# Issuing each group's value product one step later than its last transposes, in a mixed attention and retention layer

## The chip, the cores and the metric

The kernel runs on one core of a Trainium2 chip. The metric is the device time of one execution in microseconds, as the median of several runs. The engines are named as in the profile: PE is the matrix engine (PEld its weight loads), DVE the vector engine, ACT the scalar engine, POOL the general engine, and SP the engine that issues most of the DMAs.

## The reference, cut to what matters

One layer over 1024 rows of width 1024, batch 1. One input projection feeds three kinds of heads and a gate; their outputs are gated, projected back and added to the input, and a norm ends it.

```
u = rms_norm(x); proj = u @ w_in          # split into q, k, v of the groups, index keys, gate
o_a: 6 heads, causal; a = softmax(q1 k1) - lam * softmax(q2 k2); o = a @ v; norm per head
o_b: 6 heads; an index score picks 256 keys for each query (top-k); softmax over these; o = p @ v
o_c: 4 heads of retention over chunks of 128
y = silu(gate) * concat(o_a, o_b, o_c);  out = rms_norm(x + y @ w_out)
```

The change touches o_a and o_b. Both make, for each block of 128 queries, a row-wise softmax over the keys so far, transpose it (the value product wants the keys on the partitions) and multiply it with the values.

## The kernel before, in words

`diff(pair)` computes two heads of o_a, `dsa(pair, half)` two heads of o_b for one half of the queries. Both drive one generator, `attend`, with four stages of their own: `head` loads a head's queries and keys from DRAM into tiles `st`, `scores` multiplies them into a PSUM tile `pS` (L718, L787, L788), `soft` takes the row maximum on DVE out of `pS` (L729, L795) and the exponential on ACT (L731, L796), and `comb` normalises (in `diff` on POOL, L744, and DVE, L747).

`attend` walks over steps. A step is one block i of 128 queries of one head; two blocks (i = 2g and 2g+1) make a group g. Its pipeline is written out by hand. At time t it issues the scores of step t, then the transposes of step t-2 (L678, 128x128 each, up to four into one PSUM tile `pB`, L676) and the copy of each such tile into the group's SBUF tile `pt` (L679, helper lines L113 and L115, nearly always on ACT), then `comb` of step t-1 and `soft` of step t. If step t-2 was the second of its group, it then issues the group's value product (L693), which reads `pt` and the values `v`, and writes another `pB` tile. A value product has 2i+1 instructions: 15, 11, 7 or 3 for i = 7, 5, 3, 1. Groups run from the last to the first in `diff` (3, 2, 1, 0), and (1, 0) or (3, 2) in `dsa`.

All `pB` tiles share two PSUM buffers, all `pS` tiles two others, and `pt` has two. A tile of a buffer can be written only when the readers of the tile that had it before are done: for transposes that is the copy into `pt`, for a value product the copy `yo` (L519, L115) in `diff` or the multiplication by the gate `gt` (L825) in `dsa`.

What is written here is the order of issue. A scheduler that knows the dependencies, the buffers and an estimate of durations then sets the order on each engine; every engine works through its own queue in that order. Other generators are mixed with `attend` by weights: the matrix products of the input projection (`gemm`, L130 to L132, and L347 to L349), the top-k search (`topk`, on DVE and ACT, L443 to L464), the tie rule (`ties`), retention, and the output projection (`project`, L1003 to L1005). The weights apply to the costs that the generators yield, so that a generator with another number of yields is also mixed differently.

The lines that matter most are the buffers:

```
def pS(self): ... tag="S", bufs=2
def pB(self, shape=(128, 512)): ... tag="B", bufs=2
pts[g, a] = self.sb.tile([128, NB, W], F, name=self.name("pt"), tag="pt", bufs=2)
```

Of the kernel before, what the change touches and what calls it, by code (L numbers as in the profile page):

```python
# [68 lines left out]
class Trunk:  # L69
# [582 lines left out]
    def attend(self, pair, stages, GB=2, groups=(3, 2, 1, 0)):  # L652
        nc = self.nc
        steps = [(a, g, i) for a in range(2) for g in groups
                 for i in range(g * GB, g * GB + GB)]
        head, scores, soft, comb = stages
        pts, val = {}, {}
        W = GB * 128
        N = len(steps)
        hd = {}  # L660
        for t in range(N + 2):
            if t < N:
                a, g, i = steps[t]
                if a not in hd:
                    hd[a] = head(a)
                val[t] = scores(hd[a], i)
            if t >= 2:
                a, g, i = steps[t - 2]
                pr = val.pop(t - 2)
                if (g, a) not in pts:  # L670
                    pts[g, a] = self.sb.tile([128, NB, W], F, name=self.name("pt"), tag="pt", bufs=2)
                pt = pts[g, a]
                qo = (i - g * GB) * 128
                for k0 in range(0, i + 1, 4):
                    nk = min(4, i + 1 - k0)
                    p = self.pB((128, 4, 128))  # L676
                    for k in range(nk):
                        nc.tensor.transpose(p[:, k], pr[:, (k0 + k) * 128:(k0 + k + 1) * 128], self.ident)  # L678
                    self.cp(self.evac_eng[k0 // 4], pt[:, k0:k0 + nk, qo:qo + 128], p[:, :nk])  # L679
            if 0 <= t - 1 < N:  # L680
                val[t - 1] = comb(val[t - 1])
            if t < N:
                val[t] = soft(steps[t][2], val[t])
            if t >= 2 and steps[t - 2][2] % GB == GB - 1:
                a, g, i = steps[t - 2]
                o = self.pB((128, 128))
                h = 2 * pair + a
                vals = [self.v[:, k, h * 64:(h + 1) * 64] for k in range(i + 1)]
                with self.tc.manual_schedule(engines={mybir.EngineType.PE}):
                    for k in (i, *range(i)):  # L690
                        for u in (1, 0):
                            if k < i or u:
                                self.last = nc.tensor.matmul(  # L693
                                    o[u * 64:(u + 1) * 64], vals[k], pts[g, a][:, k, u * 128:(u + 1) * 128],
                                    start=k == (i if u else 0), stop=k == i - 1, skip_group_check=True)
                yield 0.5, (a, g, o)
            yield (steps[min(t, N - 1)][2] + 1) / 4.5, None
# [354 lines left out]
```

## Time and profile before

| what | value |
|---|---|
| median of 3 runs | 768.53 us (767.16 to 770.72) |
| the profiled execution, its own time | 772.95 us |
| its span, first to last instruction | 771.2 us |
| PE busy | 718.2 us, 93% |
| DVE busy | 559.9 us, 73% |
| ACT busy | 458.6 us, 59% |
| mean granted clock of PE | 0.973 |

PE is the engine with the most busy time. Its records overlap, since matrix products are pipelined: products of 128x512 show 0.39 us each and start 0.23 us apart. A product with a 32-bit operand that takes two passes has two records, so a value product of 15 instructions is shown as x30. The execution that was profiled took 4.42 us more than the median of the runs.

### The profile page before, as it was taken

Reading aid. Unit: us, or ns where it says so; the run is one execution under the profiler, and the core shown is the slowest. Engines: PE = TensorE matmul, PEld = TensorE weight load, DVE = VectorE, ACT = ScalarE, POOL = GpSimd, SP = SyncE. Lnnn points to the kernel's source line nnn. Section 1 sums busy time; section 2 is a strip of 40 time slices with the busy share of each in tenths; the row PEclk is TensorE's granted clock in tenths of the full one; section 3 lists DMA queues with packets and bytes.
Section 4 is the critical chain, followed back from the end, with each engine's and each line's share of the span. In section 5 each row is a group of like instructions: output and inputs, shape, how many; then the busy total and the mean of one; then the engine's idle time right before and its main releaser. Section 6 shows DMA issues by size and latency. Waiting matters only on the chain.

```text
span 771.2 us, 12824 instructions
## 1 busy us (share of the span) xinstructions
PE 718.2 (93%) x4266; PEld 591.1 (77%) x4266; DVE 559.9 (73%) x1315; ACT 458.6 (59%) x1002; POOL 310.4 (40%) x343
## 2 busy tenths in 40 slices
PE   6999999999989999978889889999978999999996
PEld 5986788887878988756767668989756887777884
DVE  3684577989999989999889986426657775654443
ACT  4762555489687877786845655533355665653332
POOL 6422122434424539447347787337633332120000
PEclk9999999999999999999899989999979999999998
DMA  9716455472484344451383685565579964413441
GB/s 337 255 28 178 137 159 142 111 191 79 118 202 109 99 132 113 114 144 31 91 239 108 172 229 167 145 203 165 177 212 272 251 203 113 132 34 106 137 166 55
DMA packets 93618, 116.73 MB, mean 151 GB/s; under 512 B 11120, under 2 KB 62704, under 8 KB 93424
## 3 DMA queue, kind: packets, MB, share of 16 engines
q1 hardware_dynamic: 91152, 111.94, 50.8%
q10 hardware_dynamic: 2400, 3.97, 1.4%
q8 instruction: 34, 0.56, 0.3%
q14 instruction: 32, 0.26, 0.1%
HBM read 79.17 MB, written 36.18 MB: 150 GB/s over the span
## 4 chain that ended last, share of the span: by engine, by line
PE 62%; DVE 13%; DMA 8%; issue 7%; ACT 4%; POOL 4%; SPq 2%; ACTq 0%; DVEq 0%; POOLq 0%
PE pG L130 6%; PE pG L131 6%; PE pG L132 6%; PE pB L693 5%; PE pB L678 4%; PE pG L1003 4%; PE pG L1004 4%; PE pG L1005 4%; PE pS L272 3%; PE pG L347 2%; DVE jv L443 2%; PE pG L349 2%; PE pG L348 2%; PE pS L409 2%; PE pS L408 2%
## 5 line engine op out<-in xcount | busy, mean ns | idle before, releaser
L130 PE MATMUL pG<-uh,wh 128*128 128x512 f32 x352 | 142.5, 405 | 4.5 <-DVE gt L894 2.1
L132 PE MATMUL pG<-uh,wl 128*128 128x512 f32 x352 | 141.2, 401 | 1.7 <-POOL wl L123 1.7
L131 PE MATMUL pG<-ul,wh 128*128 128x512 f32 x352 | 140.4, 399 | 1.3 <-DVE ul L255 1.3
L123 POOL TENSOR_TENSOR wl<-wr,wh 128x512 fp32r<-128x512 f32 x56 | 79.9, 1443 | 84.4 <-PE pG L131 73.8
L457 ACT ACTIVATE ja<-sc,tk_c 128x896 int8<-128x896 f32 (+2 forms) x93 | 83.3, 896 | 22.3 <-DVE tk_c L464 16.5
L113 ACT ACTIVATE pt<-pB 128x512 f32<-128x512 f32 (+2 forms) x120 | 58.9, 496 | 41.9 <-PE pB L678 41.7
L130 PEld LDWEIGHTS pG<-uh,wh 128*128 128x128 f32 x352 | 67.5, 192 | 19.3 <-DVE gt L894 2.4
L132 PEld LDWEIGHTS pG<-uh,wl 128*128 128x128 f32 x352 | 67.4, 192 | 16.7 <-POOL wl L123 2.5
L131 PEld LDWEIGHTS pG<-ul,wh 128*128 128x128 f32 x352 | 67.4, 191 | 15.5 <-DVE ul L255 3.3
L678 PE MATMUL pB<-ident,pp 128*128 128x128 f32 x432 | 73.4, 288 | 4.6 <-DVE gt L825 1.9
L693 PE MATMUL pB<-pt,v 128*64 128x128 f32 x864 | 68.0, 294 | 7.4 <-ACT pt L113 6.8
L693 PEld LDWEIGHTS pB<-pt,v 128*64 128x64 f32 x864 | 55.3, 143 | 18.9 <-ACT pt L113 9.5
L443 DVE TENSOR_SCALAR_CACHE_REDUCE jv<-sc,tk_c 128x640 bf16<-128x640 f32 (+4 forms) x81 | 69.1, 853 | 0.9
L119 POOL TENSOR_SCALAR wh<-wr 128x512 fp32r<-128x512 f32 x56 | 40.3, 723 | 69.9 <-DMA wr<-in_w_in_dram 50.8
L678 PEld LDWEIGHTS pB<-ident,pp 128*128 128x128 f32 x432 | 51.7, 145 | 20.4 <-issue 8.5
L744 POOL TENSOR_SCALAR pq<-pq,mx 128x896 f32<-128x896 f32 (+7 forms) x48 | 39.2, 816 | 58.5 <-DVE mx L743 46.1
L347 PE MATMUL pG<-wh,uh 128*128 128x256 f32 x192 | 55.4, 290 | 0.7 <-POOL wh L119 0.7
L411 ACT ACTIVATE pp<-pS 128x1024 f32<-128x1024 f32 (+5 forms) x48 | 36.5, 760 | 31.5 <-PE pS L409 31.5
L348 PE MATMUL pG<-wl,uh 128*128 128x256 f32 x192 | 55.0, 287 | 0.0
L349 PE MATMUL pG<-wh,ul 128*128 128x256 f32 x192 | 54.4, 284 | 0.0
L747 DVE SCALAR_TENSOR_TENSOR pp<-pp,mx,pq 128x896 f32<-128x896 f32 (+7 forms) x48 | 51.1, 1065 | 4.4 <-POOL pq L744 3.6
L416 DVE SCALAR_TENSOR_TENSOR sc<-pp,iw,sc 128x1024 f32<-128x1024 f32 (+5 forms) x42 | 43.5, 1048 | 14.6 <-ACT pp L411 14.2
(234 smaller groups left out, 1731.4 us busy)
## 6 DMA issues: line engine op xcount, KB each, us to landing
wr<-in_w_in_dram SPq DMA_DIRECT2D x56, 256.0 KB, 3.1
st<-qdq SPq DMA_DIRECT2D x24, 256.0 KB, 4.2
st<-qkk SPq DMA_DIRECT2D x18, 256.0 KB, 6.1
qiq<-hl SPq DMA_DIRECT2D x16, 256.0 KB, 3.5
st<-qiq SPq DMA_DIRECT2D x8, 512.0 KB, 3.4
wr<-in_w_out_dram SPq DMA_DIRECT2D x16, 256.0 KB, 3.3
xr<-in_x_dram SPq DMA_DIRECT2D x8, 512.0 KB, 3.6
yr<-yd SPq DMA_DIRECT2D x7, 512.0 KB, 4.1
```

Source lines behind the costliest of these rows:

```text
L113: self.nc.scalar.activation(out, in_, AF.Copy)
L123: (self.nc.vector if e2 == "v" else self.nc.gpsimd).tensor_tensor(lo, src, hi.bitcast(F), OP.subtract)
L130: mm(ps, wh, xh, start=start, stop=False)
L131: mm(ps, wh, xl, start=False, stop=False)
L132: mm(ps, wl, xh, start=False, stop=stop)
L347: mm(ps, uh, hs[k], start=k == 0, stop=False)
L348: mm(ps, uh, ls[k], start=False, stop=False)
L349: mm(ps, ul, hs[k], start=False, stop=k == KC - 1)
L443: nc.vector.tensor_scalar(jv[:, :nv[b]], hb if b == 7 and bit >= 16 else sc[b], t, 0.0, op0=op, op1=OP.add, accum_out=cnt[:, j:j + 1])
L457: nc.scalar.activation(ja[:, :nv[b]], sc[b], AF.Sign, bias=cut(b), scale=-1.0, accum_out=cnt[:, cols[b]:cols[b] + 1])
L678: nc.tensor.transpose(p[:, k], pr[:, (k0 + k) * 128:(k0 + k + 1) * 128], self.ident)
L693: self.last = nc.tensor.matmul(o[u * 64:(u + 1) * 64], vals[k], pts[g, a][:, k, u * 128:(u + 1) * 128], start=k == (i if u else 0), stop=k ...
```

## The change

The loop of `attend` runs one step longer. Where the value product of a group was issued in the same step as the group's last transposes, the group is now only noted (`done`), and its product is issued at the same place of the next step (`ready`), that is behind the scores, the transposes, `comb` and `soft` of that next step. `L` names the distance of two steps between scores and transposes, which stays. Each `attend` yields once more.

```diff
-        for t in range(N + 2):
+        L = 2
+        done = None
+        for t in range(N + L + 1):
             if t < N:
                 a, g, i = steps[t]
                 if a not in hd:
                     hd[a] = head(a)
                 val[t] = scores(hd[a], i)
-            if t >= 2:
-                a, g, i = steps[t - 2]
-                pr = val.pop(t - 2)
+            ready, done = done, None
+            if L <= t < N + L:
+                a, g, i = steps[t - L]
+                pr = val.pop(t - L)
                 if (g, a) not in pts:
                     pts[g, a] = self.sb.tile([128, NB, W], F, name=self.name("pt"), tag="pt", bufs=2)
                 pt = pts[g, a]
...
                     self.cp(self.evac_eng[k0 // 4], pt[:, k0:k0 + nk, qo:qo + 128], p[:, :nk])
+                if i % GB == GB - 1:
+                    done = (a, g, i)
             if 0 <= t - 1 < N:
                 val[t - 1] = comb(val[t - 1])
             if t < N:
                 val[t] = soft(steps[t][2], val[t])
-            if t >= 2 and steps[t - 2][2] % GB == GB - 1:
-                a, g, i = steps[t - 2]
+            if ready:
+                a, g, i = ready
                 o = self.pB((128, 128))
```

Both programs hold the same instructions; what differs is their order on every engine. Three places are shown. In the change's rows the lines behind L661 have moved by a few: L681 is the transposes (L678 before), L698 the value product (L693), L723 the scores (L718).

**Place 1** is PE at the first value product (15 instructions) of the second head of `diff(1)`. The names `pG` are products of other generators. Before:

```order
L678 MATMUL pB_3346<-ident,pp_3215 128x128 x4
L678 MATMUL pB_3352<-ident,pp_3215 128x128 x4
L718 MATMUL pS_3463<-st_3128,st_3125 128x384
L132 MATMUL pG_3573<-uh,wl_3488 128x512
L130 MATMUL pG_3573<-uh,wh_3487 128x512
L131 MATMUL pG_3573<-ul,wh_3487 128x512
L132 MATMUL pG_3573<-uh,wl_3488 128x512
L718 MATMUL pS_3510<-st_3121,st_3118 128x512
L693 MATMUL pB_3370<-pt_3298,v_158 64x128 x15
L678 MATMUL pB_3466<-ident,pp_3319 128x128 x4
```

And in the change:

```order
L681 MATMUL pB_3377<-ident,pp_3230 128x128 x4
L681 MATMUL pB_3383<-ident,pp_3230 128x128 x4
L723 MATMUL pS_3438<-st_3106,st_3103 128x384
L506 MATMUL pG_3425<-hl_3422,ct 128x512
L723 MATMUL pS_3440<-st_3113,st_3110 128x384
L681 MATMUL pB_3443<-ident,pp_3308 128x128 x4
L681 MATMUL pB_3449<-ident,pp_3308 128x128
L723 MATMUL pS_3516<-st_3106,st_3103 128x512
L698 MATMUL pB_3464<-pt_3287,v_158 64x128 x15
L723 MATMUL pS_3518<-st_3113,st_3110 128x512
```

The five transposes of the next step now stand ahead of the product, and the four products of the input projection that stood between have gone elsewhere. The product takes the PSUM buffer of the four transposes `pB_3443` before it.

**Place 2** is PE at the second value product (11 instructions) of the first head of `diff(1)`. Before, ten products of the input projection stand between its last two transposes and the score product shown first here:

```order
L131 MATMUL pG_3288<-ul,wh_3278 128x512
L132 MATMUL pG_3288<-uh,wl_3279 128x512
L718 MATMUL pS_3071<-st_2484,st_2481 128x256
L693 MATMUL pB_2977<-pt_2882,v_158 64x128 x11
L678 MATMUL pB_3039<-ident,pp_2901 128x128 x3
L678 MATMUL pB_3073<-ident,pp_2974 128x128 x4
```

In the change twenty-one products of the input projection and a score product stand between those two transposes and the three of the next step, shown in the third row:

```order
L130 MATMUL pG_3233<-uh,wh_3170 128x512
L681 MATMUL pB_3020<-ident,pp_2878 128x128 x3
L698 MATMUL pB_3037<-pt_2859,v_158 64x128 x11
L723 MATMUL pS_3117<-st_3106,st_3103 128x512
L723 MATMUL pS_3117<-st_3106,st_3103 128x384
```

The product moved behind the next step's transposes and further away from its own.

**Place 3** is the queue of SP around the loads of the second head of `diff(1)` (`st`, L383). The stores `qsq` (L370) write a projection that `dsa` needs later, out of tiles `hl` that POOL fills. Before:

```order
L522 DMA yo_64<-yo_2790 64x128 x2
L370 DMA qsq_3169<-hl_3238 64x2x512 x2
L383 DMA st_3118<-qdq_1854 64x1024 x2
L370 DMA qsq_3169<-hl_3272 64x2x512 x2
L383 DMA st_3121<-qdk_1647 64x1024
L383 DMA st_3121<-qdk_1647 32x1024 x2
L530 DMA f_2906<-gd_1398 128x512
L383 DMA st_3125<-qdq_1854 64x1024 x2
```

And in the change:

```order
L522 DMA yo_64<-yo_2900 64x128 x2
L383 DMA st_3103<-qdq_1890 64x1024 x2
L900 DMA gr<-gt_3163 128x512
L383 DMA st_3106<-qdk_1673 64x1024
L383 DMA st_3106<-qdk_1673 32x1024 x2
L383 DMA st_3110<-qdq_1890 64x1024 x2
L383 DMA st_3113<-qdk_1673 64x1024
L530 DMA f_2921<-gd_1398 128x512
```

The loads no longer stand behind the two stores.

## Rows read from the trace of the kernel before

**Rows 1.** The page's busy times and its slices (PEclk is the granted clock).

```profile
PE 718.2 (93%) x4266; PEld 591.1 (77%) x4266; DVE 559.9 (73%) x1315; ACT 458.6 (59%) x1002; POOL 310.4 (40%) x343
...
PEclk9999999999999999999899989999979999999998
```

**Rows 2.** Busy us of each engine by stretch, with clock and DMA share.

```profile
core 0: us, PE busy (x) PEld busy (x) DVE busy (x) ACT busy (x) POOL busy (x), PEclk, DMA share, GB/s
...
300.00:350.00 50.00, 42.61 (x244) 32.56 (x242) 47.95 (x118) 41.74 (x99) 28.99 (x32) 1.00 0.47 128
350.00:400.00 50.00, 43.25 (x244) 35.09 (x242) 43.93 (x119) 33.12 (x78) 24.58 (x27) 0.93 0.43 111
```

**Rows 3.** What PE waited for: us in total, times, longest.

```profile
PE pB L693 <- ACT pt L113: 6.8, 3, 3.5
...
PE pS L718 <- DVE mx L729: 4.6, 8, 0.9
```

**Rows 4.** PE in order of time around place 1: start, us, work, idle before.

```profile
362.36 1.03 PE L678 MATMUL pB<-ident,pp 128*128 128x128 f32 x8
...
364.12 0.40 PE L132 MATMUL pG<-uh,wl 128*128 128x512 f32 x1
364.35 0.39 PE L130 MATMUL pG<-uh,wh 128*128 128x512 f32 x1
...
365.04 0.46 PE L718 MATMUL pS<-st,st 128*128 128x512 f32 x1
369.01 3.67 PE L693 MATMUL pB<-pt,v 128*64 128x128 f32 x30 [3.51 <-ACT pt L113]
372.61 1.12 PE L678 MATMUL pB<-ident,pp 128*128 128x128 f32 x4
```

**Rows 5.** ACT in the same stretch.

```profile
363.82 0.94 ACT L731 ACTIVATE pp<-pp,mx 128x768 f32<-128x768 f32 x1 [3.53 <-DVE mx L729]
...
366.35 1.03 ACT L457 ACTIVATE ja<-sc,tk_c 128x896 int8<-128x896 f32 x1
...
367.90 1.06 ACT L113 ACTIVATE pt<-pB 128x512 f32<-128x512 f32 x2
```

**Rows 6.** DVE behind it.

```profile
374.16 0.29 DVE L729 CUSTOM_DVE_ANT_0 pq<-pS,cb 128x128 f32<-128x128 f32 x1 [1.74 <-PE pS L718]
...
379.91 0.69 DVE L729 CUSTOM_DVE_ANT_0 pp<-pS,cb 128x512 f32<-128x512 f32 x1 [0.93 <-PE pB L678]
```

**Rows 7.** PE clock in two stretches, columns as in the second group.

```profile
366.95:373.80 6.85, 4.79 (x35) 4.46 (x36) 5.43 (x14) 6.63 (x18) 2.71 (x4) 0.50 0.38 107
...
561.50:571.80 10.30, 9.25 (x40) 6.55 (x41) 6.28 (x25) 6.33 (x20) 4.29 (x4) 0.50 0.59 180
```

**Rows 8.** PE around place 2.

```profile
309.83 1.96 PE L693 MATMUL pB<-pt,v 128*64 128x128 f32 x30
...
325.30 0.38 PE L678 MATMUL pB<-ident,pp 128*128 128x128 f32 x2
...
327.85 0.28 PE L718 MATMUL pS<-st,st 128*128 128x256 f32 x1
330.90 1.52 PE L693 MATMUL pB<-pt,v 128*64 128x128 f32 x22 [2.78 <-ACT pt L113]
...
335.22 0.65 PE L718 MATMUL pS<-st,st 128*128 128x512 f32 x2 [1.02 <-DMA st<-qdk]
```

**Rows 9.** SP's issues in the same stretch (place 3).

```profile
327.76 1.28 SPq L370 DMA_DIRECT2D qsq<-hl  x2
329.09 2.15 SPq L383 DMA_DIRECT2D st<-qdk  x3
```

**Rows 10.** PE at a value product of the first half of `dsa`.

```profile
550.58 0.65 PE L693 MATMUL pB<-pt,v 128*64 128x128 f32 x6 [0.47 <-ACT pt L113]
```

**Rows 11.** PE at the last value product.

```profile
708.39 1.06 PE L678 MATMUL pB<-ident,pp 128*128 128x128 f32 x7
710.07 1.50 PE L693 MATMUL pB<-pt,v 128*64 128x128 f32 x22 [0.61 <-DVE pt L115]
```

**Rows 12.** ACT in the same stretch.

```profile
709.14 0.60 ACT L113 ACTIVATE pt<-pB 128x512 f32<-128x512 f32 x1 [0.17 <-PE pB L678]
```

## The prediction, made before the changed kernel ran

> **What bounds the kernel now.** I read the page first: PE is busy for 93% of the span and DVE for 73% [rows 1]. The reader should not stop at the average. The table by stretch shows that between 300 and 400 us DVE is the fuller engine at first: 47.95 of 50 us, with PE at 42.61 [rows 2]. There the softmaxes of `diff` share DVE with the top-k search, and PE idles because its scores and copies come late. Later it is PE that is full.
>
> Then I asked what PE waits for. The wait that the change is about, the value product waiting for the copy of its transposes, heads the list with 6.8 us, but that is three waits [rows 3]: 2.78 us at 330.90 [rows 8], 3.51 us at 369.01 [rows 4], and 0.47 us at 550.58 [rows 10]. A fourth, for a copy that DVE made, is 0.61 us at 710.07 [rows 11]. Together 2.78 + 3.51 + 0.47 + 0.61 = 7.37 us, or 1.0% of the time. There are 60 value products; the other 56 found their copy made, since the order had already put other work between.
>
> Why was the copy late at 369 us? The eight transposes ended at 362.36 + 1.03 = 363.39; the copies ran from 367.90 to 368.96 [rows 4, 5]. That is 5.57 us, of which the copies are 1.06. ACT was not short of time: it had stood 3.53 us for an exponential whose row maximum DVE had not made, and only then went through its queue, in which the copies come behind that exponential and the top-k's `ja` [rows 5]. The cause is DVE, and a product issued later doesn't change it. With no such queue the copy ends soon: at the last group it ran from 709.14 to 709.74, right behind transposes that ended by 709.45 [rows 11, 12].
>
> After the wait the PE clock is at its lower level, 1.2 GHz: 0.50 granted from 366.95 to 373.80, with 4.79 us of work in it [rows 7]. The same kind of product took 3.67 us there [rows 4] and 1.96 us at the full clock [rows 8]. Half of 4.79, 2.4 us, is the price.
>
> **The change part by part.** *Work.* No instruction is added or removed but for the engine of a few `pt` copies, each about 0.6 us [rows 12]: zero. What moves is order, on every engine.
>
> *Place 1, the 3.51 us wait.* In the change the product is behind the next step's five transposes. It writes the PSUM buffer that four of these have just filled, so it must wait until they are copied away. Only one transpose and one score product are between, about 0.1 + 0.23 = 0.34 us by the spacing of products (364.12 to 364.35 [rows 4]; a transpose of 128 columns is taken as less than half of that). Before, four products of the projection and two score products stood between. So the product still waits for a copy on ACT, of later transposes, behind other exponentials. The wait lies between 0.6 - 0.34 = 0.3 us (the quick copy) and 5.57 - 0.34 = 5.2 us (the slow one). The row at this very place is the nearest, so I keep 3.5 us: term 0, between -3.2 and +1.7. What of it reaches the end is what it takes from DVE, which stood 1.74 and 0.93 us after it [rows 6]: a gain of at most 2.7 us, not the 3.51.
>
> *Place 2, the 2.78 us wait.* Here the order does help. The copy was done at 330.90, which is 330.90 - 325.68 = 5.2 us after the transposes. In the change twenty-one projection products, a score product and three transposes stand between, (21 + 1) x 0.23 + 0.3 = 5.4 us, and the buffer it needs is an older one. I expect the wait gone. But DVE was busy for 47.95 of 50 us around it [rows 2], so the idle time of PE was not what set the end there: I take 0, between -2.8 and 0.
>
> *Place 3.* The loads of the next head stood behind `qsq` stores that left at 327.76 [rows 9], and PE waited 1.02 us for them [rows 8]. Now they go first. Under the same DVE cover: 0, between -1.0 and 0.
>
> *The two small waits.* At 710 us PE is the full engine, and in the change twenty-five products of the output projection precede the last value product; 0.61 is saved on the path. The one at 550.58 us is taken as saved too: together -1.1 us, at the worst 0.
>
> *Waits added.* Counted over the whole order, two of the six 15-instruction products of `diff` now have less than 0.8 us of work between the transposes whose buffer they take and themselves: place 1 and its like in the first head of `diff(2)` (three projection products, about 0.7 us). The second can cost up to 5.57 - 0.7 = 4.9 us, and at place 1 the five transposes follow the eight of the step before with only three small products between, so that they wait too. Under DVE's cover I take 0 for both; 4.9 is the upper end. Queued behind a waiting product are the scores of later steps, for which DVE waits; that is how it would reach the end.
>
> In the first half of `dsa`, where steps are short, the distance from the transposes whose copy or buffer gates a product to that product is about 0.2 to 1.3 us in most cases before and 0.3 to 1.2 after: the change moves nothing there. The step that each `attend` runs more only emits the product that was held back.
>
> *The sum.* 0 + 0 + 0 - 1.1 + 0 = -1.1 us on the profiled execution's 772.95, so 771.9. That execution was 4.42 us above the median of 768.53; on the median it is **767.4 us**.
>
> **The rivals.** *Faster, the waits really go.* For it: place 2 loses its wait outright, and the stretch at half clock begins in the wait at place 1. Against it: DVE is full at both, and place 1 keeps its gate. All gains together: 7.4 for the waits, 2.4 for the clock, 1.0 for the loads, 10.8 us, 757.7; what is more likely of it is DVE's 2.7 on top of the 1.1, plus one or two, so 762 to 764.
>
> *Slower, the product waits for the buffer it takes.* With two `pB` buffers a product issued behind the next step's transposes takes the buffer these have just filled. At place 1 and at its like PE would stand 1.7 us more and 4.9 us, and one more stretch at half clock costs 2.4: 9 us, 777.5. It decides as soon as DVE runs dry behind these products, as it did at 374.16 [rows 6]; while DVE has other work queued it costs nothing. For it: the order at place 1, with 0.34 us between. Against it: only two of 24 products in `diff` stand so.
>
> The Trainium skill, TensorE: Matmul & The Clock Gate, section "A second HAM failure mode: psum-queue depth-cycling", says that a matrix engine that cycles through PSUM buffers and idles a little between groups loses more than the idle time, since its clock falls and rises again. The half clock behind the wait at place 1 agrees [rows 7]; by that rule each wait for a buffer is dearer than its length, and this rival would be the likelier.
>
> *The change doesn't do what it says.* The scheduler reorders anyway, so a product issued later may stand no further from its copy, as in the first half of `dsa`. Then the time is 768.5; this is within my forecast.
>
> **How the numbers follow.** Time within 0.5% of before (764.7 to 772.4; about what a measurement of this kernel can tell from no change, its runs spanning 767.16 to 770.72) has 0.40: waits move along and DVE hides them. Faster 0.32: the order of everything else moved too, and it takes only DVE's gaps going to pass 3.9 us. Slower 0.28, the buffer wait. The likeliest case's own range is 764.7 to 772.4. The full range takes in both ends, 10 us down and 9 us up: 758.5 to 777.5; past these I leave 0.2.
>
> **What would show it.** In the changed kernel's list of PE waits, the value product should still wait for an ACT copy in `diff`, at place 1 for the copy of the following step's transposes, with about 3 us, and not at place 2 nor at the last product. Transposes should wait for copies of the step before at place 1, where none did. DVE should still be above 90% busy from 300 to 350 us. I am wrong if the waits of the value product and of the transposes together fall by several us and DVE's gaps with them, if DVE gets new gaps of 2 us behind a value product, or if another order-made difference (loads, gates, the clock in the stretch around 561 us [rows 7]) is larger than all of this.

## The result, and the profile after

The changed kernel is slower by about half a per cent. Its median is 774.54 us (771.09 to 777.70, 15 runs) against 769.82 us (767.16 to 775.42, 15 runs) of the kernel before on the same chip; the ratio is 1.0056, with a 95% interval from 1.0032 to 1.0080. The time lies inside the stated range (758.5 to 777.5). The likeliest case was a time within 0.5% of before, which the interval still reaches into, but the forecast of 767.4 us was 1.1 us faster, and the change is slower.

The two profiled executions don't show this: 773.35 us after, 772.95 before, with spans of 771.6 and 771.2 us. Executions of the kernel before lie up to 10 us apart, so a difference of 4 us is seen in medians. Single profiles can only show where PE stands idle, and the one of before was taken of an execution 4.42 us above its median. Busy times and clock of after, to be held against [rows 1]:

```profile
PE 713.4 (92%) x4266; PEld 587.2 (76%) x4266; DVE 563.6 (73%) x1316; ACT 455.3 (59%) x1001; POOL 317.6 (41%) x343
...
PEclk9999999999999999999999899999889999999999
```

```profile
core 0: 771.6 us, clock 0.980
```

PE is busy 4.8 us less in a span that is no shorter. The clock can account for all of that: it is 0.980 in the mean of this execution against 0.973, and (0.027 - 0.020) x 2 x 771 is some 11 us less at 1.2 GHz, where a product took about twice as long (3.67 us against 1.96, [rows 4, 8]), so half of these 11 us would be saved. What the clock gave back went into idle time of PE, 771.6 - 713.4 = 58.2 us against 771.2 - 718.2 = 53.0. (Over many executions the clocks of the two kernels are alike; see the last section.) The list of what PE waited for (us in total, times, longest) says where the idle time is, against [rows 3]:

```profile
PE pB L681 <- DVE gt L830: 5.6, 3, 5.1
PE pS L723 <- DMA st<-qdk: 5.4, 3, 2.8
PE pS L723 <- DVE mx L734: 5.1, 7, 1.5
PE pB L681 <- DVE pp L752: 3.9, 2, 3.3
...
PE pB L681 <- ACT pt L113: 3.6, 4, 1.6
...
PE pB L698 <- ACT pt L113: 2.0, 1, 2.0
PE pB L681 <- ACT yo L115: 1.7, 1, 1.7
```

The value product (L698) waits once, for 2.0 us, where it waited four times. The transposes (L681) now wait in its place. The page's groups give the totals; the last figures of a row are the idle time before the group's instructions and its main cause. Before:

```profile
L678 PE MATMUL pB<-ident,pp 128*128 128x128 f32 x432 | 73.4, 288 | 4.6 <-DVE gt L825 1.9
L693 PE MATMUL pB<-pt,v 128*64 128x128 f32 x864 | 68.0, 294 | 7.4 <-ACT pt L113 6.8
```

After:

```profile
L681 PE MATMUL pB<-ident,pp 128*128 128x128 f32 x432 | 69.1, 282 | 15.1 <-DVE gt L830 5.6
...
L698 PE MATMUL pB<-pt,v 128*64 128x128 f32 x864 | 68.8, 293 | 2.0 <-ACT pt L113 2.0
```

Waits of 7.4 + 4.6 = 12.0 us became 2.0 + 15.1 = 17.1. That is not yet a cause: the 5.1 us among them turns out not to be needed for the loss (below).

**The places the prediction spoke of.** Place 1, PE in order of time:

```profile
348.65 0.71 PE L681 MATMUL pB<-ident,pp 128*128 128x128 f32 x5
349.11 0.47 PE L723 MATMUL pS<-st,st 128*128 128x512 f32 x1
351.54 3.21 PE L698 MATMUL pB<-pt,v 128*64 128x128 f32 x30 [1.95 <-ACT pt L113]
```

ACT there:

```profile
349.88 1.03 ACT L457 ACTIVATE ja<-sc,tk_c 128x896 int8<-128x896 f32 x1
...
350.91 0.58 ACT L113 ACTIVATE pt<-pB 128x512 f32<-128x512 f32 x1
```

The product waits for the copy of the four transposes just ahead of it, which stands on ACT behind an exponential and the top-k's `ja`: 1.95 us, where [rows 4] had 3.51. The transposes ahead of it, at 348.65 and the eight before them at 345.48, waited for nothing, though the prediction expected them to. At place 2 (against [rows 8]) and at the last value product (against [rows 11]) it no longer waits:

```profile
318.04 0.49 PE L681 MATMUL pB<-ident,pp 128*128 128x128 f32 x3
318.45 1.52 PE L698 MATMUL pB<-pt,v 128*64 128x128 f32 x22
```

```profile
708.85 0.40 PE L1010 MATMUL pG<-woh,yr 128*128 128x512 f32 x1
709.18 1.52 PE L698 MATMUL pB<-pt,v 128*64 128x128 f32 x22
```

By stretch, against [rows 2], DVE is as full as it can be from 300 to 350 us:

```profile
300.00:350.00 50.00, 44.49 (x257) 34.19 (x255) 49.58 (x129) 43.19 (x103) 25.74 (x26) 1.00 0.45 117
350.00:400.00 50.00, 44.56 (x245) 34.99 (x245) 46.75 (x119) 34.59 (x82) 30.79 (x32) 0.97 0.50 131
```

In these 100 us after does more, and it is some 4 us ahead when the first head of `diff(1)` ends (last value product at 342.7 us, before at 346.7). So whatever is lost is lost later.

**Where PE idles more.** Behind the last score product of `diff`, two things are left for PE to mix in the main: products of the input projection, which wait for nothing much, and the first half of `dsa`, whose steps are short chains through ACT and DVE. I cut the trace at that score product, at the last projection product, and at the last value product of that half. Before:

```profile
492.40:548.40 56.00, 55.09 (x457) 50.93 (x458) 22.78 (x67) 18.06 (x49) 26.77 (x37) 1.00 0.58 179
548.40:586.80 38.40, 32.67 (x206) 23.17 (x206) 26.56 (x89) 23.30 (x62) 14.61 (x16) 0.82 0.79 226
```

After:

```profile
496.30:542.90 46.60, 45.60 (x369) 42.44 (x367) 21.43 (x59) 13.82 (x40) 22.41 (x32) 1.00 0.58 184
542.90:587.40 44.50, 32.53 (x221) 23.61 (x220) 33.35 (x93) 24.48 (x66) 20.96 (x22) 0.85 0.75 220
```

While projection products last, PE stands for 1 us in all. When they are used up, `dsa` has nothing beside it, and PE idles 38.40 - 32.67 = 5.7 us before and 44.50 - 32.53 = 12.0 us after. In the order of instructions on PE, 336 projection products are left behind the last score product of `diff` before, and 291 after. The other 45 were issued earlier. In this pair of profiles the half of `dsa` ends at the same time, 586.8 and 587.4 us, since both executions took the same time; the idle time is where the change leaves PE without work, not yet a measured loss.

### The profile page after: what moved, and what is told of

Its sections match the earlier page's. It is cut to its first block, busy times and chain, and to the rows that moved or that the text cites. A ratio compares the mean times of both kernels' runs of the same rounds, so it can differ in the third digit from the quotient of the medians.

```text
span 771.6 us, 12842 instructions
## 1 busy us (share of the span) xinstructions
PE 713.4 (92%) x4266; PEld 587.2 (76%) x4266; DVE 563.6 (73%) x1316; ACT 455.3 (59%) x1001; POOL 317.6 (41%) x343
## 4 chain that ended last, share of the span: by engine, by line
PE 54%; DVE 24%; DMA 9%; issue 7%; POOL 3%; ACT 3%; SPq 1%; DVEq 0%; ACTq 0%; POOLq 0%
DVE jv L443 6%; PE pB L698 4%; PE pG L1008 4%; PE pG L130 4%; PE pG L1009 4%; PE pG L1010 4%; PE pG L131 4%; PE pG L132 4%; DVE pp L752 3%; PE pB L681 3%; PE pS L272 3%; PE pG L347 2%; PE pG L348 2%; PE pG L349 2%; DVE pp L734 2%
## 5 line engine op out<-in xcount | busy, mean ns | idle before, releaser
L132 PE MATMUL pG<-uh,wl 128*128 128x512 f32 x352 | 139.2, 395 | 0.5 <-POOL wl L123 0.5
L113 ACT ACTIVATE pt<-pB 128x512 f32<-128x512 f32 (+2 forms) x120 | 57.8, 493 | 43.4 <-PE pB L681 43.1
L681 PE MATMUL pB<-ident,pp 128*128 128x128 f32 x432 | 69.1, 282 | 15.1 <-DVE gt L830 5.6
L681 PEld LDWEIGHTS pB<-ident,pp 128*128 128x128 f32 x432 | 50.8, 143 | 27.4 <-DVE gt L830 6.5
L749 POOL TENSOR_SCALAR pq<-pq,mx 128x896 f32<-128x896 f32 (+7 forms) x48 | 48.1, 1003 | 56.7 <-DVE mx L748 47.3
L698 PE MATMUL pB<-pt,v 128*64 128x128 f32 x864 | 68.8, 293 | 2.0 <-ACT pt L113 2.0
L698 PEld LDWEIGHTS pB<-pt,v 128*64 128x64 f32 x864 | 54.8, 142 | 14.6 <-issue 5.7
L723 PE MATMUL pS<-st,st 128*128 128x512 f32 (+3 forms) x144 | 43.8, 369 | 11.2 <-DMA st<-qdk 5.4
```

The source lines that it names most:

```text
L113: self.nc.scalar.activation(out, in_, AF.Copy)
L132: mm(ps, wl, xh, start=False, stop=stop)
L698: self.last = nc.tensor.matmul(o[u * 64:(u + 1) * 64], vals[k], pts[g, a][:, k, u * 128:(u + 1) * 128], start=k == (i if u else 0), stop=k ...
```

## The experiments

Each was timed in turns with the kernel before on the same chip; a ratio is to that kernel, with its 95% interval.

**The error of the measurement, and the change again.** `null_before` is the kernel before, unchanged; `late_again` is the change, unchanged.

> The kernel before, unchanged, as a control. Every theory expects a ratio of 1.000 within its interval (0.998 to 1.002) and a median near 769.8 us; what the interval misses by tells how far a difference of half a per cent can be trusted. Its profile is a second one of the same program: the waits of the value product for the copy should again sum to about 7 us, if they belong to the program and not to one execution.

Measured: 1.0007 [0.9984, 1.0030]; two of the same cannot be told apart within 0.25%.

> The changed kernel once more, for a second profile and a second measurement of its ratio. Every theory expects a ratio of 1.003 to 1.008. Theory 1 expects the wait of about 5 us of the transposes for gt in the first half of dsa to be in this profile too, and PE busy at most 40 of 50 us there; if it is gone, it belonged to one execution.

Measured: 1.0038 [1.0007, 1.0068]. Slower again. The 5.1 us wait of the transposes for `gt` is there again with 4.9.

**Half of the change.** `attend` takes a parameter, and the other callers set it to 0:

```diff
-        for t in range(N + L + 1):
+        for t in range(N + L + lag):
...
-            ready, done = done, None
+            ready, done = (done, None) if lag else (None, None)
...
-                    done = (a, g, i)
+                    if lag:
+                        done = (a, g, i)
+                    else:
+                        ready = (a, g, i)
```

> The product is one step late in diff only; dsa is as before. Theory 1 (the loss is made in the first half of dsa, where the late product's PSUM buffer is freed by the gate multiplication, which stands in DVE's queue behind splits of the output weights): no slower than before, 766 to 770 us, with the waits of the value product in diff mostly gone and no 5 us wait of the transposes for gt. Theory 2 (the buffer wait of my prediction, in diff): about 774 us. Theory 3 (any reordering costs about half a per cent, wherever it is made): somewhere between 768 and 776, with new waits at other places.

Measured: 1.0031 [1.0007, 1.0056].

> The product is one step late in dsa only; diff is as before. Theory 1: 773 to 776 us, with a wait of transposes for gt of several us in the first half of dsa and PE busy below 40 of the 50 us there (38.0 in the changed kernel, 42.6 before). Theory 2: 768 to 771 us. Theory 3: between 768 and 776.

Measured: 1.0033 [1.0014, 1.0053]. Each half costs about half of what the change lost. Each also has the added yield of its own `attend`, so neither is lateness alone. The part in `diff` was the surprise, since the waits at place 2 go there too.

> The product one step late in the first half of dsa only. Theory 1 (late products in that half block the transposes until the gate multiplication is done): ratio 1.003 or more, as late_in_dsa (1.0033). If the second half makes the loss: 0.998 to 1.002. Lottery theory: 1.003 to 1.006 in either half.

Measured: 1.0017 [0.9998, 1.0036], not clear of 1.

**The buffer the product takes.** `late_ahead` issues the held-back product of the step before ahead of the new step's transposes (the block moves up with its yield, behind `ready, done = done, None`). `own_step_pg` and `late_pg` give it a buffer that it doesn't share with transposes, in the kernel before and in the change:

```diff
-                o = self.pB((128, 128))
+                o = self.pG((128, 128))
```

> The product is one step late everywhere, but issued ahead of the next step's transposes, so that it takes the older of the two buffers and the transposes wait for its reader. Theory 1: still slow, 772 to 776 us, since the reader is the same gate multiplication and now gates the very next transposes. Theory 2: 766 to 769 us, since the product no longer waits for the buffer that was just filled. Theory 3: between 768 and 776.

Measured: 1.0116 [1.0092, 1.0140], worse than behind them. In its list of waits the value product leads, since the last copies are no earlier and less work stands between:

```profile
PE pB L679 <- ACT pt L113: 10.2, 5, 3.5
```

> As before (product in its own step), but the product writes one of the two PSUM buffers of the matrix products (pG) and no longer one of the two of the transposes. Control for late_pg; the matrix products now share their buffers with the value products, so that any theory allows 765 to 785 us.

Measured: 1.0689 [1.0649, 1.0730].

> The change, with the product in a pG buffer. Buffer theory (a late product and the transposes compete for the two pB buffers, and that is what being late costs): late_pg is no slower than own_step_pg, or faster by 0.3% or more, since being late then only gives the copy more time. If being late costs by itself (order, later release of pt, later gates): late_pg is slower than own_step_pg by about 0.5%, as in the pair with pB.

Measured: 1.0695 [1.0656, 1.0735]. The `pG` buffers are those of the projections, and taking them costs 7% either way. But the two are equal within their intervals: there the whole change, added yield included, shows neither gain nor loss above some 0.4%. With `pG` setting the time, this pair cannot say what the shared buffer costs in the change.

**The added step alone.** `yield_only` has the longer loop, but issues each product in its own step as before; no product is late:

```diff
-            ready, done = done, None
+            ready = None
...
-                    done = (a, g, i)
+                    ready = (a, g, i)
```

> The loop runs one step longer and yields once more for each attend, but every value product is issued in its own step, as before. The order differs from the second pair of diff on. If the loss comes from products issued late (theory 1 or 2): 768 to 771 us, ratio 0.998 to 1.002. If it comes from the other mixing of the generators (theory 3): 772 to 775 us, a ratio of 1.003 to 1.006, without any late product.

Measured: 1.0058 [1.0030, 1.0085]. That is the whole loss, with no late product at all. Its value product waits 8.9 us and its transposes only 3.1, less than the 4.6 of before, so the loss doesn't need their wait of 5 us for `gt`:

```profile
L698 PE MATMUL pB<-pt,v 128*64 128x128 f32 x864 | 66.4, 290 | 8.9 <-ACT pt L113 8.3
L681 PE MATMUL pB<-ident,pp 128*128 128x128 f32 x432 | 71.6, 284 | 3.1 <-DVE gt L830 1.0
```

Its two stretches, cut at the same three events:

```profile
499.80:543.50 43.70, 42.96 (x351) 40.31 (x351) 19.93 (x53) 12.09 (x34) 22.41 (x33) 1.00 0.61 190
543.50:587.40 43.90, 30.69 (x225) 21.63 (x225) 33.32 (x97) 25.70 (x70) 20.99 (x22) 0.92 0.75 218
```

They are after's shape again: 13.2 us idle in the second (43.90 - 30.69). The reverse holds the product back, but does not yield the added step:

```diff
-            yield (steps[min(t, N - 1)][2] + 1) / 4.5, None
+            if t < N + L:
+                yield (steps[min(t, N - 1)][2] + 1) / 4.5, None
```

> The change as it is, except that the added last step of each attend yields no cost, so that the generators are mixed by the same number of yields as before. Yield theory (the loss is the one more yield, as yield_only with 1.0058 says): ratio 0.997 to 1.002, about 770 us. Lateness theory (a late product costs by itself): 1.004 or more, 774 us. Lottery theory (any other order than the tuned one costs about half a per cent): also 1.003 to 1.006, whatever is changed.

Measured: 1.0028 [1.0006, 1.0049]: about half of the loss gone, though the interval overlaps with the change's. It lies between what the yield theory and the lateness theory had said, and decides for neither.

> The product one step late in diff only, and no added yield. If yields cost 0.6% and lateness in diff gains what late_in_diff lacks to that (1.0031 against 1.0058): ratio about 0.997, 768 us, faster than both kernels. Lottery theory: 1.003 to 1.006.

This has the product late in `diff` only, and no added yield. Measured: 1.0006 [0.9987, 1.0024]. Lateness in `diff` shows no cost and no gain. The 0.997 that was expected if lateness in `diff` gains by itself did not come. The waits did not vanish, though; they moved from the product to the transposes, 3.2 + 9.8 = 13.0 us where the kernel before had 12.0:

```profile
L681 PE MATMUL pB<-ident,pp 128*128 128x128 f32 x432 | 71.4, 283 | 9.8 <-ACT pt L113 5.1
L701 PE MATMUL pB<-pt,v 128*64 128x128 f32 x864 | 66.0, 285 | 3.2 <-ACT pt L113 2.3
```

**Why a yield costs.** The mixer always takes the generator with the least yielded cost for its weight; the three `diff` have weight 36. One `diff` yields 2 x 36 / 4.5 = 16 for its steps, 8 x 0.5 for its products and 2 x 2 / 4.5 = 0.9 at its end, 20.9 in all. The added yield is 2 / 4.5 = 0.44 more, 2.1%, for no work (each half of `dsa` yields once more too). `diff` then counts as further on than it is, and the others run ahead, as they would at a weight of 36 / 1.021 = 35.3. If that is the mechanism, the weight alone must do the same. The edit is `'wd': 36` to 35 in the kernel before, and to 37 in both:

> The kernel before with diff's weight 35 in place of 36. One more yield per diff makes it count as further on than it is, so that it is held back against the other generators, as a smaller weight does (36 x 20.9 / 21.3 = 35.3). Yield theory, share of diff as the cause: ratio 1.003 to 1.006, as yield_only (1.0058). If only the added place where others are put between costs, or the exact order: 0.997 to 1.002, or any value without relation to wd37 (0.9983).

Measured: 1.0054 [1.0029, 1.0079]. The weight alone makes the same loss, with the loop and every product as before.

> The kernel before with diff's weight in the mixing 37 in place of 36, and nothing else: about the same shift of the shares as one more yield of 0.44 on some 21 per diff (2%). Yield theory (diff held back or ahead against the other generators is what costs): a ratio of 1.003 to 1.007, or one below 1 if the shift goes the other way. Lottery theory: 1.003 to 1.006. Lateness theory: 0.998 to 1.002.

Measured: 0.9983 [0.9962, 1.0005], not clear of 1.

> The change with diff's weight 37, which gives back the share that the added yield takes. Yield theory, share as the cause: ratio about 1.003, as late_no_yield (1.0028), what is left being the late product in dsa. Otherwise: 1.004 to 1.006 as the change itself.

Measured: 0.9982 [0.9952, 1.0011]. The changed kernel with one number given back is no slower than before, and cannot be told from `before_wd37`; the 1.003 that was expected did not come either. Its stretches, cut as above, in a profile of its fastest execution (765.13 us, where its median is 768.98):

```profile
481.00:538.80 57.80, 57.80 (x484) 54.52 (x484) 21.11 (x64) 17.96 (x49) 27.73 (x38) 1.00 0.57 179
538.80:573.60 34.80, 30.04 (x215) 21.76 (x215) 27.87 (x91) 22.11 (x63) 13.56 (x18) 0.90 0.85 242
```

The projection lasts 57.8 us, and `dsa` stands alone for 34.8, with 4.8 idle.

**The 5.13 us wait in `dsa`.** My first theory after the result was another one, and the change's trace made it look good. PE, then DVE, then ACT around it:

```profile
550.78 0.66 PE L610 MATMUL pG<-rt,rt 128*64 128x128 f32 x8
556.57 1.97 PE L681 MATMUL pB<-ident,pp 128*128 128x128 f32 x8 [5.13 <-DVE gt L830]
```

```profile
555.54 0.69 DVE L123 TENSOR_TENSOR wol<-wr,woh 128x512 fp32r<-128x512 f32 x1 [3.07 <-ACT woh L113]
556.22 0.49 DVE L830 TENSOR_TENSOR gt<-pB,gt 128x128 f32<-128x128 f32 x2
```

```profile
554.88 0.63 ACT L113 ACTIVATE woh<-wr 128x512 fp32r<-128x512 f32 x1 [3.01 <-DMA wr<-in_w_out_dram]
```

The transposes want a buffer that the gate's multiplication must free. That one stands in DVE's queue behind the split of an output weight, which waits on ACT for a load from DRAM. If the late product makes this, taking the splits off DVE must cure it; the edit is `'oe': ('av', 'gg')` to `('ag', 'gg')`, which gives them to POOL, in both kernels:

> The kernel before with the output weights' split done on POOL instead of DVE, so that no gate multiplication stands in DVE's queue behind a split that waits for a DMA. Control for late_oe; POOL takes about 1.3 us for what DVE does in 0.7, eight times. 768 to 776 us by any theory.

Measured: 0.9965 [0.9937, 0.9993].

> The change with the output weights' split on POOL. Theory 1 (the late products of dsa cost because their buffer is freed by a gate multiplication behind these splits): late_oe is within 0.25% of before_oe, the rest being the yield, and the 5 us wait of the transposes for gt is gone from its profile. If it stays 0.4 to 0.6% above before_oe, the splits are not the cause and the 5 us wait is made up elsewhere.

Measured: 1.0131 [1.0103, 1.0160]. The theory fell: the wait of 5 us is gone, and the kernel is slower still. Its stretches:

```profile
497.60:544.50 46.90, 45.60 (x370) 42.52 (x370) 21.67 (x59) 13.88 (x40) 22.56 (x33) 1.00 0.59 183
544.50:590.30 45.80, 35.26 (x216) 26.11 (x216) 25.31 (x84) 23.50 (x64) 26.05 (x27) 0.74 0.65 192
```

These are after's lengths once more, now at a granted clock of 0.74 in the second; the profile is of its slowest execution (784.30 us, where its median is 780.23). The share of the mixer was still the change's, so I gave that back too:

> The change with both settings: weight 37 and the splits of the output weights on POOL. 371 products of the input projection are left behind the last scores of `diff`, as in late_wd37 and 80 more than in late_oe. If late_oe lost its 1.3% because the added yield left too few of these products, the two gains are independent and this one is about 0.9982 x 0.9965 = 0.995 (0.991 to 0.998) of before. If the splits on POOL disagree with the late product itself (its copies, the loads behind it), it stays over 1.005, near late_oe's 1.0131.

Measured: 0.9991 [0.9966, 1.0017]. With the share given back, the loss of `late_oe` is gone.

> The kernel before with the same two settings and the product in its own step; 369 products are left. By the theory of the mixing share it is the same as late_wd37_oe within 0.3%, about 0.995 (0.991 to 0.998). If lateness gains by itself once the share is given back, late_wd37_oe is below it by more than 0.3%; if it costs by itself, above it.

Measured: 0.9993 [0.9972, 1.0014]. Late or not, no difference that the intervals of about 0.25% can tell; but the two gains don't add, and neither beats `before_oe`. That one, the kernel before with the splits on POOL, is the fastest that was found clear of 1: 767.87 us against 770.36, below both kernels of this case.

**All of them by the mixing.** `left` is the number of projection products behind the last score product of `diff`, from the order on PE; `idle` is PE's idle time, in us, from the last of them to the end of the first half of `dsa`, the second stretch above, in the one profile of each (5.7 in that of before). `own_step_pg` and `late_pg` are left out, since `pG` sets their time.

| kernel | product | left | idle | ratio |
|---|---|---|---|---|
| before_wd35 | own step | 255 | 10.1 | 1.0054 |
| yield_only | own step | 282 | 13.2 | 1.0058 |
| after; late_again | late | 291 | 12.0; 12.3 | 1.0056; 1.0038 |
| late_ahead | late, ahead of the transposes | 291 | 8.7 | 1.0116 |
| late_oe | late | 291 | 10.5 | 1.0131 |
| late_in_diff | late in diff | 291 | 7.1 | 1.0031 |
| late_in_dsa | late in dsa | 336 | 5.7 | 1.0033 |
| late_dsa_half0 | late in half of dsa | 336 | 6.1 | 1.0017 |
| null_before | own step | 336 | 6.8 | 1.0007 |
| before_oe | own step | 336 | 4.2 | 0.9965 |
| late_no_yield | late | 360 | 8.2 | 1.0028 |
| late_diff_no_yield | late in diff | 360 | 8.2 | 1.0006 |
| before_wd37; before_wd37_oe | own step | 369 | 9.4; 8.2 | 0.9983; 0.9993 |
| late_wd37; late_wd37_oe | late | 371 | 4.8; 5.6 | 0.9982; 0.9991 |

All with fewer than 336 lost at least 0.3%, and late or not made no difference that was measured at 369 to 371. The count is not the whole story: at 291 lie 1.0031 and 1.0131, and `late_in_dsa` at 336 and `late_no_yield` at 360 lost some 0.3% as well. The idle time orders them a little better. With 10 us or more all lost at least 0.38%, and with 5.6 or less none lost, but between these both occur. That any order but the tuned one loses is ruled out: `before_oe`, `late_diff_no_yield` and the four kernels at 369 to 371 all have another order and did not lose.

## Why the prediction was half right

The forecast had the wrong sign: 1.1 us faster, where the change is 4.7 us slower.

**What held.** Place 1 keeps its wait for the copy of the following step's transposes, in size between the bounds (1.95 us; forecast 3.5, from 0.3 to 5.2). The waits at place 2 and at the last product went. DVE was above 90% busy from 300 to 350 us. "Waits move along" came true: the totals show it, 12.0 us before, 17.1 in the change and 13.0 in `late_diff_no_yield`. The 1.0006 of that run agrees with the terms of 0, but as its waits only moved, it doesn't show what they would have been worth had they gone; the -1.1 us of the two small waits is below what any run can tell. The transposes at place 1 did not wait, against the forecast. At place 3 the loads left earlier (the first at 312.03 us, before at 324.10), but the scores that need them moved forward too and waited 2.3 us at 325.49, so nothing came of it.

**What failed is one sentence of the part on added waits:** "The step that each `attend` runs more only emits the product that was held back." It stood as the last 0 of the sum 0 + 0 + 0 - 1.1 + 0. The step also yields 0.44 of cost for no work, and this moves projection products ahead of the end of `diff`, 45 in the change and 54 in `yield_only`. Its price, measured by itself, is 0.0058 x 770 = 4.5 us (`yield_only`) or 0.0054 x 770 = 4.2 us (`before_wd35`). With it the sum would have been about +3.3 us, against 774.54 - 769.82 = 4.7 measured. That a generator with another number of yields is mixed differently was known and stood in the text on the kernel; I never asked by how much, nor what the moved products were covering. The last sign of being wrong named it in general, an "order-made difference" larger than all the waits.

**"The change moves nothing there"**, said of the first half of `dsa`, was wrong in the same way. I looked at the distances at each product, while the stretch loses its cover from outside: PE idles there 12.0 us in place of 5.7.

**The rivals.** "Slower" came true, but not by its mechanism. It wanted the product to wait for the buffer it takes, with PE 1.7 and 4.9 us later at place 1 and its like; the one wait there was shorter than before, and at its like there was none. Its second prop was the rule of the Trainium skill, TensorE: Matmul & The Clock Gate, section "A second HAM failure mode: psum-queue depth-cycling". The loss doesn't need it here: `late_again`, timed in turns with the kernel before on one chip, had a clock of 0.977 in the mean against 0.976, and was slower all the same. "Faster" failed because the waits did not go but moved to the transposes, and because the added yield costs more than place 2 and the loads could give.

A slip of count: I wrote of 60 value products. There are 48, 24 in `diff` and 24 in `dsa`, so 44 others had found their copy made; no term used it.

**What stays open.** First, lateness in `dsa`. `late_in_dsa` cost 0.33% at weight 36, but it has the added yields of `dsa` too (0.44 of cost in each first half, 1.33 in each second). Without them, lateness in `dsa` is what sets `late_no_yield` (1.0028) apart from `late_diff_no_yield` (1.0006), and these intervals overlap. At weight 37 late or not agree within the intervals of some 0.3%, which could hide as much.

Second, why `late_oe` and `late_ahead` lost more than 1%. For `late_ahead` no run tells. Giving the share back removes the loss of `late_oe`, but that share alone costs 0.5%. These two also had a lower clock than the kernels timed together with them, 0.970 and 0.972 in the mean of their executions against 0.977 for the kernel before beside each; for `late_oe` that is some 10 us more at 1.2 GHz. Whether that is a cause or comes of idle time was not tested.

Third, that idle PE in the first half of `dsa` is the path by which the share acts is argued, not shown. It fits the traces of after, `yield_only`, `before_wd35` and `late_wd37`; but `before_wd37` has 9.4 us idle there and lost nothing, and `late_in_dsa` lost with 5.7:

```profile
543.60:585.00 41.40, 31.96 (x219) 22.93 (x217) 29.07 (x93) 24.95 (x66) 15.81 (x19) 0.88 0.81 229
```

## What to carry to other kernels

When instructions are mixed by a budget (weights, costs, due times), a loop that runs once more spends budget even where it issues nothing: price the step itself, and look for the work that it pushes away from the stretch it was covering. A control with the new bookkeeping and the old order (here `yield_only`) belongs among the first runs, before any theory on waits. And ask of each wait that a change removes where it goes: the value product lost 5.4 of its 7.4 us of waits, and the transposes gained 10.5.

## What was not expected of the hardware

Executions of the unchanged kernel lay between 766.80 and 776.65 us, 1.3% apart, so a profile of each kernel could not have shown the loss.

The clock varied with them, and the two profiles misled me. They show 0.973 before and 0.980 after, as if the slower kernel had the better clock. Over all executions whose clocks are known there is no such difference: 0.975 and 0.977 in the mean for the change (15 and 12 executions), and 0.976 to 0.978 for the kernel before (six sets of 12 to 35). Within one kernel a lower clock goes with a longer time: of the 15 executions of the change, the five fastest had 0.977 in the mean and the five slowest 0.971.
